# A Mamba scan inside a two-layer trunk: the decay work behind the last Silu, the first scan step two items later, another bank for the first feature, the last group's items in a new order

## The chip, the cores and the metric

One core of a Trainium2 chip runs the whole program in one launch. The metric is device microseconds (us) of one execution; lower is better. Engines are named as the profile names them: PE (TensorE, its weight loads as PEld), DVE (VectorE), ACT (ScalarE), POOL (GpSimd) and SP (SyncE, which here only issues transfers). Each engine takes its instructions in one fixed order, and an instruction that waits holds up all behind it.

## What is computed

The reference is a trunk of two pre-norm layers on 256 tokens of width 2048, in float32: a Mamba-2 mixer, an MLP, a dilated attention, an MLP and a last norm. The change touches the Mamba mixer alone. Cut to what matters:

```python
zxbcdt = u @ w_in                                 # z 4096, xbc 6144, dt 64 columns
xbc = silu(causal_depthwise_conv(xbc, conv_w, conv_b))
xs, bm, cm = split(xbc)                           # 8 groups of 512, 128 and 128 columns
L  = segsum_exp(dt * A)                           # decays inside a chunk of 128 tokens
cb = einsum("bclgn,bcsgn->bcgls", cm, bm)
y  = einsum("bcgls,bgjcls,bcsgjp->bclgjp", cb, L, x) + y_off     # y_off: state of the chunk before
y  = (y + d_skip * xs) * silu(z)
y  = per-group rms norm of y * norm_w
return y @ w_out
```

## The kernel before, in words

**Weights.** Each weight unit is a tile of 128x2048 floats (1 MB). SP loads it into a raw buffer, ACT copies it with rounding into `wh`, the high part (L267), DVE subtracts the two into `wl`, the low part (L268), and PE multiplies with both (`fetch`, L219). There are three pairs of `wh`/`wl`, used in turn. So the `wh` of a unit may be written only when PE has finished the unit three places before, and a raw buffer is loaded again only when the `wl` made from it is done. From the third group on plain units share two raw buffers; the third is tile A, and there is a tile B.

**Groups.** The mixer works through eight groups of heads. A group has six features (`c0` to `c3` for x, `c4` for B, `c5` for C; 32 matmuls each, L295), and four quarters of its gate (`z0` to `z3`, 24 matmuls each, L330 to L332). A feature's bank is emptied (`c_ux`, `c_ut`), convolved with four taps (`c_ua`, L533 and L535) and put through a Silu (`c_uo`, L538). The gate's two banks are read by the two `zs` Silus (L613).

**Scan.** Each group's scan has three steps, and the steps of one group lie in different places. `first` (item `f`, L616) fetches the rows of cumulated decays (`ab<-acs_rows`, a transfer issued by ACT), multiplies B with C on PE (`cb`, L633), takes Abs of each of 16 blocks with the head's offset as bias (L643) and Exp of both halves (L648) on ACT, multiplies them with `cb` on DVE (L650), and transposes the features (`xt`, `bt`) with five products on DVE (`xdt`, `xd`, `xdd`). `second` runs in the next group: `y` (L693) up to the first half's output, and `Y` with the state's part (`yo`). `third` (`t`) transposes the result. Item `p` makes from two groups the seven operands (`op`, L754, L755) of a seven-product scheme for the output projection.

**Output projection.** Items `1` to `7` are those seven products (12 matmuls, L785). Each adds up in a bank that DVE then adds to the residual `x_res` (L793). Products `5` and `3` use bank 3, `1`, `6`, `7` and `4` bank 2. Their weights are made in tiles A and B by adding transfers issued by POOL, except for `1`, `3` and `2`, which SP loads. Items `o60` to `o73` are the plain projection of the last two groups.

**Order.** The table `GROUP_ORDER` (L50) writes out by hand the order of the items in each group. From group 3 on, PE's order is pinned to it (`put_in_order`, L553), as is the chain of all `wh` and `wl`. The other instructions on ACT and DVE are placed by a scheduler that works with modelled times; `tc.issue_after` forbids it to place an instruction ahead of another.

Of the kernel before, what the change touches and what calls it, by code (L numbers as in the profile page):

```python
# [10 lines left out]
AF = mybir.ActivationFunctionType  # L11
# [5 lines left out]
NH = S // P  # L17
# [5 lines left out]
HG = 8  # L23
# [17 lines left out]
def alibi_slope(g, h):  # L41
# [6 lines left out]


GROUP_ORDER = {  # L50
    1: "c0 c1 c2 c3 c4 y Y c5 z0 z1 z2 z3 t f",
    2: "c0 c1 c2 y Y c3 c4 c5 t f z0 p z1 z2 z3",
    **{g: "c0 c1 1 c2 y c3 Y 5 c4 3 c5 t 6 z0 7 f z1 2 z2 4 z3" + " p" * (g % 2 == 0) for g in range(3, 7)},
    7: "c0 c1 1 c2 y c3 Y 5 c4 3 c5 t 6 z0 7 f z1 2 z2 4 z3",
    8: "1 o60 y o61 Y 5 o62 3 o63 t 6 7 o70 2 o71 4 o72 o73",
}
GROUP_ORDER = {g: order.split() for g, order in GROUP_ORDER.items()}

# [55 lines left out]
def hybrid_trunk_kernel(ctx: ExitStack, tc: tile.TileContext, a: dict, out: bass.AP):  # L114
    nc = tc.nc
# [24 lines left out]
    def bank(name, among):  # L140
        k = banks_of.use(banks_of.peek(among))
        return psum.tile([P, 512], F32, tag=f"b{k}", name=name, bufs=1)
# [264 lines left out]
    def ssm(nx):  # L407
# [9 lines left out]
        for j in range(4):  # L417
            n = KT if j == 0 else 0
            if j == 0:
                t, sq = sp.tile([P, n + 4 * S], F32, tag="B", name="xt0_0", bufs=1), None  # L420
                g0 = t[:, :KT]
            else:
                t, sq = (sp.tile([P, 4 * S], F32, tag="op", name=f"xt{k}_{j}", bufs=7) for k in range(2))
# [37 lines left out]
        sm = {}  # L461
# [61 lines left out]
        y3, silus = {}, []  # L523
# [29 lines left out]
        def put_in_order(make):  # L553

            if not fixed[0]:
                return make()
            with tc.issue_after(latest[0]):
                return make()
# [5 lines left out]
        class Group:  # L564
# [30 lines left out]
            def features(self, u):  # L595
                g, name = self.g, f"c{self.g}_{u}"
                unit = lambda made=None: cols_units([("in", g, u)], xs, [name], first=(u != 1 if g >= 3 else u < 2),
                                                     made=made)[0]
                ps = put_in_order(lambda: unit([bank(name, (0, 1))] if g >= 3 else None))
                self.ch.append(conv_tile(g, u, ps))  # L600

            def gate(self, q):
# [13 lines left out]
            def first(self):  # L616
                g, ch = self.g, self.ch
                ab = sp.tile([P, NH, HG, P], F32, tag="ab", name=f"ab{g}", bufs=1)
                rows = sm["scratch"][:, g * HG * P:(g + 1) * HG * P]
                nc.scalar.dma_start(ab.rearrange("p m h t -> p m (h t)"),  # L620
                                    rows.unsqueeze(0).to_broadcast([P, NH, HG * P]))
                hs = slice(g * HG, (g + 1) * HG)
                bT, cT = ch[4], ch[5]

                def bc(v):
                    return v.unsqueeze(2).to_broadcast([P, HG, HD])

                def heads(t):
                    return t.rearrange("p (h d) -> p h d", h=HG)

                ps = sm_bank(f"cb{g}")
                halves = [slice(m * P, (m + 1) * P) for m in range(NH)]
                small(lambda: [nc.tensor.matmul(ps[:, t], bT[:, t], cT[:, t], start=(t.start == 0), stop=True,  # L633
                                                skip_group_check=True) for t in halves])
                cb = sp.tile([P, NH, P], F32, tag="cb", name=f"cbm{g}", bufs=1)
                nc.vector.tensor_tensor(cb, ps[:, :S].rearrange("p (m l) -> p m l", m=NH),
                                        tri[:, None, :].to_broadcast([P, NH, P]), ALU.mult)

                es = [ab[:, m] for m in range(NH)]
                for m in range(NH):  # L640
                    for h in range(HG):
                        av = sm["less"][:, m, g * HG + h:g * HG + h + 1]
                        nc.scalar.activation(es[m][:, h], es[m][:, h], AF.Abs, bias=av)  # L643
                with ExitStack() as order:
                    for ins in silus[-2:]:
                        order.enter_context(tc.issue_after(ins))
                    for m in range(NH):
                        nc.scalar.activation(es[m], es[m], AF.Exp, scale=-1.0)  # L648
                for m in range(NH):
                    nc.vector.tensor_tensor(es[m], es[m], cb[:, m:m + 1, :].to_broadcast([P, HG, P]),  # L650
                                            ALU.mult)

                xdt, xd = [], []
                for m in range(NH):
                    ps = sm_bank(f"xt{g}_{m}")
                    small(lambda: [nc.tensor.transpose(ps[:, c * P:(c + 1) * P], ch[c][:, halves[m]], ident)
                                   for c in range(4)])
                    t = sp.tile([P, GW], F32, tag="xdt", name=f"xdt{g}_{m}", bufs=2)
                    nc.vector.tensor_tensor(heads(t), heads(ps), bc(sm["dt"][:, m, hs]), ALU.mult)
                    xdt.append(t)  # L660
                    t = sp.tile([P, GW], F32, tag="xd", name=f"xd{g}_{m}", bufs=2)
                    nc.vector.tensor_tensor(heads(t), heads(ps), bc(dskip[:, hs]), ALU.mult)
                    xd.append(t)
                    if m == 0:
                        t = sp.tile([P, GW], F32, tag="yo", name=f"xdd{g}", bufs=1)
                        nc.vector.tensor_tensor(heads(t), heads(ps), bc(sm["ddt"][:, hs]), ALU.mult)
                        xdd = split(t, GW, "xdd", f"xdds{g}")
                ps = sm_bank(f"bt{g}")
                small(lambda: [nc.tensor.transpose(ps[:, :P], bT[:, :P], ident)])
                btok = split(ps[:, :P], P, "bs", f"btok{g}")  # L670
                cs = split(cT[:, P:], P, "bs", f"cs{g}")
                self.kept = es, xdt, xd, xdd, btok, cs
# [72 lines left out]
        def operands(pair):  # L745


            left, right = slice(0, P), slice(P, S)
            y0, y1 = y3[2 * pair], y3[2 * pair + 1]
            a11, a21, a12, a22 = y0[:, :, left], y0[:, :, right], y1[:, :, left], y1[:, :, right]  # L750
            of = {k: sp.tile([P, 4, 2, P], F32R, tag="op", name=f"op{pair}_{k}", bufs=7) for k in "1536724"}

            def parts(k, t):
                nc.scalar.activation(of[k][:, :, 0], t, AF.Copy)  # L754
                nc.vector.tensor_tensor(of[k][:, :, 1], t, of[k][:, :, 0].bitcast(F32), ALU.subtract)  # L755

            parts("1", a11)
            parts("4", a22)
            nc.vector.tensor_tensor(a22, a21, a22, ALU.subtract)
            parts("5", a22)  # L760
            nc.vector.tensor_tensor(a21, a11, a21, ALU.add)
            nc.vector.scalar_tensor_tensor(a11, a22, -1.0, a11, op0=ALU.mult, op1=ALU.subtract)
            parts("2", a12)
            nc.vector.scalar_tensor_tensor(a12, a12, -1.0, a11, op0=ALU.mult, op1=ALU.subtract)
            parts("3", a12)
            parts("6", a11)
            parts("7", a21)
            return of
# [24 lines left out]
            nc.vector.tensor_tensor(xc, xc, ps, op)  # L793

        def plain(g, j):
            banks = [bank(f"wo{g}_{j}_{m}", (0, 1)) for m in range(NH)]
            lhs = lambda k, part, t: y3[g][t.start // P][:, k, part]
            put_in_order(lambda: rows_unit(banks, [("out", g, j)], lhs, 0, 4, 512, True, True))
            add_residual(banks, j)
            if g == 7:  # L800
                step_on(nx, j)
# [9 lines left out]
        for g, order in GROUP_ORDER.items():  # L811
            before = cur
            cur = Group(g)
            fixed[0] = g >= 3
            for item in order:
                if item[0] == "c":
                    cur.features(int(item[1]))
                elif item[0] == "z":
                    cur.gate(int(item[1]))
                elif item == "y":  # L820
                    rest = before.second()
                    next(rest)
                elif item == "Y":
                    next(rest, None)
                elif item == "t":
                    before.third()
                elif item == "f":
                    cur.first()
                elif item == "p":
                    of[(g - 2) // 2] = operands((g - 2) // 2)  # L830
                elif item[0] == "o":
                    plain(int(item[1]), int(item[2]))
                else:
                    product((g - 3) // 2, item, "ab"[(g - 3) % 2])
# [437 lines left out]
```

## Time and profile before

| what | value |
|---|---|
| median of 3 runs | 2603.98 us (2600.7 to 2606.12) |
| profiled execution, its own time | 2602.75 us |
| span of its trace | 2601.0 us |
| mean granted TensorE clock | 0.985 |
| busy PE, DVE, ACT | 2532.7, 2058.6, 1602.2 us |
| Mamba mixer, from the start to about | 757 us |

A row of the timeline gives start, duration, engine, line, operation and tiles, and in brackets how long the engine had been idle and what ended that. A row that ends in x4 stands for four instructions in a line. The granted clock is the share of full speed that PE was given.

### The profile page before, as it was taken

Reading aid. Unit: us, or ns where it says so; the run is one execution under the profiler, and the core shown is the slowest. Engines: PE = TensorE matmul, PEld = TensorE weight load, DVE = VectorE, ACT = ScalarE, POOL = GpSimd, SP = SyncE. Lnnn points to the kernel's source line nnn. Section 1 sums busy time; section 2 is a strip of 40 time slices with the busy share of each in tenths; the row PEclk is TensorE's granted clock in tenths of the full one; section 3 lists DMA queues with packets and bytes.
Section 4 is the critical chain, followed back from the end, with each engine's and each line's share of the span. In section 5 each row is a group of like instructions: output and inputs, shape, how many; then the busy total and the mean of one; then the engine's idle time right before and its main releaser. Section 6 shows DMA issues by size and latency. Waiting matters only on the chain.

```text
span 2601.0 us, 34411 instructions
## 1 busy us (share of the span) xinstructions
PE 2532.7 (97%) x13737; PEld 2176.2 (84%) x13737; DVE 2058.6 (79%) x2296; ACT 1602.2 (62%) x1991; POOL 119.8 (5%) x143
## 2 busy tenths in 40 slices
PE   9998989987999999999999999999999999999998
PEld 7887867776788888888888999999988888888887
DVE  8777777677678988889886766667767988899885
ACT  7776566566456656666665666666656666666664
POOL 0000000000000000000000000000000000000001
PEclk9999989998999999999999999999999999999999
DMA  8556757666668888898875444455458888998883
GB/s 310 192 186 173 247 179 208 197 207 210 168 250 220 259 258 252 248 262 255 254 217 203 170 168 164 162 173 172 166 218 228 248 252 248 258 267 253 252 235 140
DMA packets 83696, 567.43 MB, mean 218 GB/s; under 512 B 9296, under 2 KB 9936, under 8 KB 20048
## 3 DMA queue, kind: packets, MB, share of 16 engines
q1 hardware_dynamic: 65232, 441.50, 47.0%
q0 software_dynamic: 15552, 113.25, 22.4%
q10 hardware_dynamic: 2752, 10.49, 1.2%
q8 instruction: 108, 1.77, 0.3%
q14 instruction: 52, 0.43, 0.0%
HBM read 563.04 MB, written 2.16 MB: 217 GB/s over the span
## 4 chain that ended last, share of the span: by engine, by line
PE 77%; DMA 2%; ACT 1%; DVE 1%; issue 0%; ACTq 0%; POOLq 0%; POOL 0%
PE h L295 27%; PE qk L295 10%; PE pxb L1089 6%; PE pxa L1089 6%; PE pwb L1089 3%; PE pwa L1089 3%; PE v L330 2%; PE v L331 2%; PE v L332 2%; PE c L295 2%; PE pzb L1089 1%; PE pza L1089 1%; PE d L330 1%; PE d L331 1%; PE d L332 1%; PE s L860 1%
## 5 line engine op out<-in xcount | busy, mean ns | idle before, releaser
L268 DVE TENSOR_TENSOR wl<-raw,wh 128x2048 fp32r<-128x2048 f32 (+4 forms) x368 | 796.7, 2167 | 299.4 <-ACT wh L267 298.2
L267 ACT ACTIVATE wh<-raw 128x2048 fp32r<-128x2048 f32 (+4 forms) x368 | 669.8, 1822 | 397.9 <-PE h L295 80.8
L295 PE MATMUL h<-xn,wh 128*128 128x512 f32 x2048 | 690.1, 392 | 0.0
L295 PE MATMUL h<-xn,wl 128*128 128x256 f32 x2048 | 555.5, 280 | 0.0
L295 PEld LDWEIGHTS h<-xn,wh 128*128 128x128 f32 x2048 | 376.4, 188 | 76.1
L295 PEld LDWEIGHTS h<-xn,wl 128*128 128x128 f32 x2048 | 385.0, 188 | 13.8
L295 PE MATMUL c<-xn,wh 128*128 128x512 f32 x768 | 263.5, 394 | 0.3 <-ACT wh L267 0.2
L295 PE MATMUL qk<-xn,wh 128*128 128x512 f32 x768 | 259.3, 393 | 0.0
L295 PE MATMUL c<-xn,wl 128*128 128x256 f32 x768 | 211.4, 283 | 5.0 <-ACT zs L613 2.5
L295 PE MATMUL qk<-xn,wl 128*128 128x256 f32 x768 | 209.2, 283 | 0.0
L295 PEld LDWEIGHTS c<-xn,wh 128*128 128x128 f32 x768 | 142.2, 188 | 31.8 <-ACT wh L267 2.6
L295 PEld LDWEIGHTS qk<-xn,wh 128*128 128x128 f32 x768 | 141.1, 188 | 28.8
L295 PEld LDWEIGHTS c<-xn,wl 128*128 128x128 f32 x768 | 144.0, 188 | 10.6 <-DVE wl L268 3.5
L295 PEld LDWEIGHTS qk<-xn,wl 128*128 128x128 f32 x768 | 141.4, 188 | 3.6 <-issue 1.2
L267 ACT ACTIVATE wh<-Ab 128x2048 fp32r<-128x2048 f32 x42 | 80.4, 1915 | 72.6 <-DMA Ab<-in_w 60.0
L268 DVE TENSOR_TENSOR wl<-Ab,wh 128x2048 fp32r<-128x2048 f32 x42 | 96.1, 2287 | 14.0 <-ACT wh L267 14.0
L267 ACT ACTIVATE wh<-Aa 128x2048 fp32r<-128x2048 f32 x42 | 80.3, 1913 | 38.6 <-DMA Aa<-in_w 30.6
L268 DVE TENSOR_TENSOR wl<-Aa,wh 128x2048 fp32r<-128x2048 f32 x42 | 96.1, 2288 | 7.4 <-ACT wh L267 7.3
L331 PE MATMUL z<-wl,xn 128*128 128x512 f32 x256 | 101.0, 394 | 0.0
L330 PE MATMUL z<-wh,xn 128*128 128x512 f32 x256 | 101.0, 399 | 0.0
L332 PE MATMUL z<-wh,xn 128*128 128x512 f32 x256 | 100.7, 394 | 0.0
L1038 ACT ACTIVATE r<-r 128x256 f32<-128x256 f32 x128 | 52.2, 411 | 73.0 <-DVE r L1037 73.0
(471 smaller groups left out, 4998.5 us busy)
## 6 DMA issues: line engine op xcount, KB each, us to landing
raw<-in_w SPq DMA_DIRECT2D x172, 1024.0 KB, 5.2
raw<-in_w_in SPq DMA_DIRECT2D x74, 1024.0 KB, 4.9
raw<-in_w_qk SPq DMA_DIRECT2D x48, 1024.0 KB, 4.8
Aa<-in_w POOLq DMA_DIRECT2D x28, 1024.0 KB, 9.6
Ab<-in_w POOLq DMA_DIRECT2D x28, 1024.0 KB, 9.9
raw<-in_w_v SPq DMA_DIRECT2D x32, 768.0 KB, 4.3
A<-in_w_out POOLq DMA_DIRECT2D x18, 1024.0 KB, 8.9
raw<-in_w_out SPq DMA_DIRECT2D x14, 1024.0 KB, 7.4
```

The source lines that it names most:

```text
L267: high[i] = nc.scalar.activation(wh[:, c], raw[:, c], AF.Copy).ins
L268: low[i] = nc.vector.tensor_tensor(wl[:, c], raw[:, c], wh[:, c].bitcast(F32), ALU.subtract).ins
L295: latest[0] = nc.tensor.matmul(ps[:, :n], (wh, wl)[part][:, kt * P:(kt + 1) * P], xs[:, kt, :, :].rearrange("p a t -> p (a t)")[:, :n], st ...
L330: nc.tensor.matmul(banks[m][:, :n], hi, wh[:, c], start=st, stop=False)
L331: nc.tensor.matmul(banks[m][:, :n], hi, wl[:, c], start=False, stop=False)
L332: latest[0] = nc.tensor.matmul(banks[m][:, :n], lo, wh[:, c], start=False, stop=sp).ins
L860: latest[0] = nc.tensor.matmul(ps[:, at:at + nk], qa[g, hl][:, qs], k[g, hl][:, :nk], start=first and at == 0, stop=not first, skip_group_ ...
L1038: nc.scalar.activation(t, t, AF.Square)
L1089: latest[0] = nc.tensor.matmul(ps, lhs(i, part), w[:, n], start=(first and i == 0 and part == 0 and w is wh), stop=(i == 3 and part == 1), ...
```

## The change

Six edits, all in the Mamba mixer:

1. The 16 Abs of `first` move into the block that may only be issued behind the last two Silus of the features, each half's Abs ahead of its Exp.
2. From group 3 to 7 item `f` stands behind `z1` and `2` and no longer ahead of them.
3. `Y` stands behind `5` in groups 3 to 7. In group 1 both halves of the second step stand behind `c5`, in group 2 `Y` behind `c3`.
4. From group 3 on `c0` uses bank 3 and no longer one of banks 0 and 1; so does the first bank of `o60`.
5. Group 8 has its items in another order: `y` right behind `1`, `t` ahead of `3`, and products between the plain units.
6. The operands of `p` may only be issued behind the last Silu.

```diff
-    **{g: "c0 c1 1 c2 y c3 Y 5 c4 3 c5 t 6 z0 7 f z1 2 z2 4 z3" + " p" * (g % 2 == 0) for g in range(3, 7)},
+    **{g: "c0 c1 1 c2 y c3 5 Y c4 3 c5 t 6 z0 7 z1 2 f z2 4 z3" + " p" * (g % 2 == 0) for g in range(3, 7)},
...
-    8: "1 o60 y o61 Y 5 o62 3 o63 t 6 7 o70 2 o71 4 o72 o73",
+    8: "1 y o60 Y o61 5 o62 t 3 o63 6 o70 7 o71 2 4 o72 o73",
...
-                ps = put_in_order(lambda: unit([bank(name, (0, 1))] if g >= 3 else None))
+                ps = put_in_order(lambda: unit([bank(name, (0, 1) if u else (3,))] if g >= 3 else None))
...
-                for m in range(NH):
-                    for h in range(HG):
-                        av = sm["less"][:, m, g * HG + h:g * HG + h + 1]
-                        nc.scalar.activation(es[m][:, h], es[m][:, h], AF.Abs, bias=av)
                 with ExitStack() as order:
                     for ins in silus[-2:]:
                         order.enter_context(tc.issue_after(ins))
                     for m in range(NH):
+                        for h in range(HG):
+                            av = sm["less"][:, m, g * HG + h:g * HG + h + 1]
+                            nc.scalar.activation(es[m][:, h], es[m][:, h], AF.Abs, bias=av)
                         nc.scalar.activation(es[m], es[m], AF.Exp, scale=-1.0)
...
-            banks = [bank(f"wo{g}_{j}_{m}", (0, 1)) for m in range(NH)]
+            banks = [bank(f"wo{g}_{j}_{m}", (3,) if g == 6 and j + m == 0 else (0, 1)) for m in range(NH)]
...
-                    of[(g - 2) // 2] = operands((g - 2) // 2)
+                    with tc.issue_after(silus[-1]):
+                        of[(g - 2) // 2] = operands((g - 2) // 2)
```

**Place one.** ACT's order in group 4, from the transfer of the decay rows to the high part of product `3`'s weights, which are in tile B. Before:

```order
L620 DMA ab_3183<-acs_rows 128x2x1024
L710 ACTIVATE ssq_junk,sq_0_2885<-xd_0_2514 128x512
L643 ACTIVATE ab_3183<-ab_3183,acs 128x128 x4
L533 ACTIVATE c_2a<-upad_191,vecs 128x256
L643 ACTIVATE ab_3183<-ab_3183,acs 128x128 x9
L313 ACTIVATE c_3x<-c_3_2893 128x256
L538 ACTIVATE c_1o<-c_1a,vecs 128x256
L713 ACTIVATE xd_0_2514<-xd_0_2514,rq_0_2887 128x512
L267 ACTIVATE wh_2961<-B_2960 128x2048
```

The same stretch of ACT in group 4 in the changed kernel:

```order
L620 DMA ab_3232<-acs_rows 128x2x1024
L709 ACTIVATE ssq_junk,sq_0_2885<-xd_0_2563 128x512
L533 ACTIVATE c_2a<-upad_191,vecs 128x256
L267 ACTIVATE wh_2946<-B_2945 128x2048
L313 ACTIVATE c_3x<-c_3_2893 128x256
```

The 13 Abs, which read what the transfer brings, no longer stand between the transfer and the weights of `3`, and three further pieces now follow those weights.

**Place two.** ACT's order in group 4 around the last feature's Silu, `c_5o`. The first row of both pieces is the high part of item `2`; the next `wh` from a raw buffer is that of `z2`, and the one from tile A (L262) that of item `4`. Before:

```order
L267 ACTIVATE wh_3165<-raw_3164 128x2048
L538 ACTIVATE c_4o<-c_4a,vecs 128x256
L754 ACTIVATE op_5_3374<-yT_3099 128x4x128
L754 ACTIVATE op_2_3378<-yT_3099 128x4x128
L267 ACTIVATE wh_3242<-raw_3241 128x2048
L538 ACTIVATE c_5o<-c_5a,vecs 128x256
L648 ACT_TABLE_LOAD
L648 ACTIVATE ab_3183<-ab_3183 128x1024 x2
```

In the changed kernel:

```order
L267 ACTIVATE wh_3165<-raw_3164 128x2048
L538 ACTIVATE c_4o<-c_4a,vecs 128x256
L538 ACTIVATE c_5o<-c_5a,vecs 128x256
L646 ACTIVATE ab_3232<-ab_3232,acs 128x128 x16
L753 ACTIVATE op_1_3373<-yT_2396 128x4x128
L267 ACTIVATE wh_3184<-raw_3183 128x2048
L753 ACTIVATE op_4_3379<-yT_3099 128x4x128
L647 ACT_TABLE_LOAD
L647 ACTIVATE ab_3232<-ab_3232 128x1024 x2
L262 ACTIVATE wh_3214<-A_2671 128x2048
```

`c_5o` now stands ahead of the high part of `z2`, and all 16 Abs behind `c_5o`. The high part of `4` has the Abs, the table load and both Exps ahead of it. In odd groups, which have no `p`, the two `op` rows are missing.

DVE's order at the same place, from the low part of `z2` on. Before:

```order
L268 TENSOR_TENSOR wl_3243<-raw_3241,wh_3242 128x2048
L636 TENSOR_TENSOR cbm_3188<-cb_3185,vecs 128x256
L659 TENSOR_TENSOR xdt_0_3215<-xt_0_3210,dta 128x512
L662 TENSOR_TENSOR xd_0_3217<-xt_0_3210,vecs 128x512
L666 TENSOR_TENSOR xdd_3219<-xt_0_3210,dec 128x512
```

In the changed kernel:

```order
L268 TENSOR_TENSOR wl_3185<-raw_3183,wh_3184 128x2048
L754 TENSOR_TENSOR op_4_3379<-yT_3099,op_4_3379 128x4x128
L792 TENSOR_TENSOR x_res<-x_res,qz0b 128x512
L636 TENSOR_TENSOR cbm_3237<-cb_3234,vecs 128x256
L658 TENSOR_TENSOR xdt_0_3264<-xt_0_3259,dta 128x512
L661 TENSOR_TENSOR xd_0_3266<-xt_0_3259,vecs 128x512
L665 TENSOR_TENSOR xdd_3268<-xt_0_3259,dec 128x512
L658 TENSOR_TENSOR xdt_1_3278<-xt_1_3273,dta 128x512
L661 TENSOR_TENSOR xd_1_3280<-xt_1_3273,vecs 128x512
L758 TENSOR_TENSOR yT_3099<-yT_2396,yT_3099 128x4x128
L649 TENSOR_TENSOR ab_3232<-ab_3232,cbm_3237 128x1024 x2
L263 SCALAR_TENSOR_TENSOR wl_3215<-A_2671,wh_3214 128x2048
```

Both kernels put the products of `f` ahead of the low part of `4` (L263). Since `f` now comes two items later on PE, it comes right ahead of `z2`, with `4` the next item but one.

More of the change, by code (lines that the diff above doesn't have):

```diff
@@ L50 @@
 GROUP_ORDER = {
-    1: "c0 c1 c2 c3 c4 y Y c5 z0 z1 z2 z3 t f",
-    2: "c0 c1 c2 y Y c3 c4 c5 t f z0 p z1 z2 z3",
-    **{g: "c0 c1 1 c2 y c3 Y 5 c4 3 c5 t 6 z0 7 f z1 2 z2 4 z3" + " p" * (g % 2 == 0) for g in range(3, 7)},
-    7: "c0 c1 1 c2 y c3 Y 5 c4 3 c5 t 6 z0 7 f z1 2 z2 4 z3",
-    8: "1 o60 y o61 Y 5 o62 3 o63 t 6 7 o70 2 o71 4 o72 o73",
+    1: "c0 c1 c2 c3 c4 c5 y z0 Y z1 z2 z3 t f",
+    2: "c0 c1 c2 y c3 Y c4 c5 t f z0 p z1 z2 z3",
+    **{g: "c0 c1 1 c2 y c3 5 Y c4 3 c5 t 6 z0 7 z1 2 f z2 4 z3" + " p" * (g % 2 == 0) for g in range(3, 7)},
+    7: "c0 c1 1 c2 y c3 5 Y c4 3 c5 t 6 z0 7 z1 2 f z2 4 z3",
+    8: "1 y o60 Y o61 5 o62 t 3 o63 6 o70 7 o71 2 4 o72 o73",
 }
```

## The prediction

> **What bounds the kernel now.** The windows of the profile come first: group 3 to 6 (each from the item behind `c2` to the same place one group later), group 7, group 8, the rest. The columns are the stretch, its us, the busy time of PE, PEld, DVE, ACT and POOL, the granted clock, DMA's share and GB/s.
>
> ```profile
> 220.07:313.32 93.25, 83.40 (x466) 69.36 (x464) 68.46 (x76) 57.29 (x74) 5.14 (x7) 0.96 0.72 219
> 313.32:409.06 95.74, 84.89 (x465) 71.36 (x464) 71.63 (x85) 58.25 (x77) 4.92 (x7) 0.93 0.66 198
> 409.06:498.45 89.39, 83.68 (x465) 69.88 (x464) 66.00 (x75) 55.24 (x72) 4.98 (x7) 0.96 0.71 212
> 498.45:593.50 95.05, 84.83 (x465) 71.23 (x464) 71.66 (x85) 58.18 (x77) 5.00 (x7) 0.93 0.66 199
> 593.50:683.11 89.61, 75.70 (x394) 61.93 (x392) 58.26 (x73) 50.44 (x69) 4.48 (x6) 0.89 0.61 182
> 683.11:760.00 76.89, 74.61 (x406) 61.59 (x405) 60.99 (x72) 43.93 (x61) 4.49 (x6) 0.98 0.72 222
> 760.00:2601.00 1841.00, 1831.46 (x9872) 1590.51 (x9870) 1486.28 (x1571) 1118.80 (x1315) 86.18 (x94) 1.00 0.73 222
> ```
>
> PE is the bound everywhere. From 760 on it idles 9.5 of 1841 us, so nothing is to be had there, and the change doesn't touch it. In groups 3 to 7 it idles 5.7 to 13.9 us a group, and the clock falls to 0.89 to 0.96. The waits of PE between 220 and 683 say on what (total, times, longest):
>
> ```profile
> PE cb L633 <- ACT c_5o L538: 17.7, 3, 6.2
> PE qw0a L785 <- DVE x_res L793: 5.7, 1, 5.7
> PE qw0b L785 <- ACT wh L267: 3.5, 1, 3.5
> PE qw2a L785 <- ACT wh L267: 3.4, 1, 3.4
> ```
>
> Two places, then: `cb` at item `f`, and product `3` (the `qw` rows, once a group). ACT stands behind both. At `3` it waits for the decay rows, five times 5.3 us; this is group 4:
>
> ```profile
> ACT ab L643 <- DMA ab<-acs_rows: 26.3, 5, 6.3
> ```
>
> ```profile
> 326.94 1.28 ACT L643 ACTIVATE ab<-ab,acs 128x128 f32<-128x128 f32 x4 [5.37 <-DMA ab<-acs_rows]
> ...
> 332.44 1.90 ACT L267 ACTIVATE wh<-B 128x2048 fp32r<-128x2048 f32 x1
> ```
>
> ```profile
> 334.39 0.80 PE L785 MATMUL qw0b<-wh,op 128*128 128x512 f32 x1 [3.48 <-ACT wh L267]
> ```
>
> The Abs wait 5.37, then 13 of them run, and only then comes `wh` of `3`, for which PE has idled 3.48. At `f`, ACT waits 2.83 for a load before it makes `wh` of `z2`, and `c_5o` stands behind that:
>
> ```profile
> 362.25 1.91 ACT L267 ACTIVATE wh<-raw 128x2048 fp32r<-128x2048 f32 x1 [2.83 <-DMA raw<-in_w_in]
> 364.06 0.49 ACT L538 ACTIVATE c_5o<-c_5a,vecs 128x256 f32<-128x256 f32 x1
> 364.57 1.28 ACT L648 ACT_TABLE_LOAD   x1
> 365.87 2.00 ACT L648 ACTIVATE ab<-ab 128x1024 f32<-128x1024 f32 x2
> ```
>
> ```profile
> 364.61 1.22 PE L633 MATMUL cb<-c_5o,c_4o 128*128 128x128 f32 x4 [5.85 <-ACT c_5o L538]
> ```
>
> A gap also costs behind its end. Product `3` of group 3, behind its gap, takes from 245.06 to 249.68, where an undisturbed product takes 2.75:
>
> ```profile
> 245.06 0.76 PE L785 MATMUL qw0a<-wh,op 128*128 128x512 f32 x1 [5.70 <-DVE x_res L793]
> ...
> 249.28 0.40 PE L785 MATMUL qw0a<-wh,op 128*128 128x512 f32 x1
> ```
>
> ```profile
> 585.37 2.75 PE qx2a L785 x12
> 588.12 5.55 PE c L295 x32
> ```
>
> (The last two are from the chain of waits: a product is 2.75, a unit of 32 matmuls 5.55.) I put this slow stretch at 1.7 us a gap.
>
> **What is lost before.** A group without gaps needs group 3's busy time less one slow stretch, 83.4 - 1.7 = 81.7; group 7, whose clock of 0.89 speaks for two or three, 75.7 - 2.5 x 1.7 = about 71.5. Window less content: 11.6, 14.0, 7.7, 13.4 and 18.1, together 64.8 us.
>
> **The change, part by part.**
>
> *Abs behind the last Silu.* Nothing is added, and the transfer of the rows is issued at the same place on ACT; SP's order stays as it is. But ACT no longer meets the transfer ahead of `3`. The old order had the Abs at 326.94 and `c_5o` at 364.06; with `c_5o` earlier by the count below, some 25 us of these 37 are left for the transfer to land, which in the old order was late by 5.4. So `wh` of `3` comes about 10 us earlier than wanted, and the gap at `3` goes. The 16 Abs now stand behind `c_5o`, for 4.8 us, as group 1 has them in a line:
>
> ```profile
> 97.72 4.80 ACT L643 ACTIVATE ab<-ab,acs 128x128 f32<-128x128 f32 x16 [1.33 <-DMA ab<-acs_rows]
> ```
>
> *`f` two items later.* `cb` needs `c_5o`, and this no longer stands behind `wh` of `z2`. To see what is late next I count from the end of `c5`'s matmuls. PE, where nothing waits: `t` 0.9, `6` 3.6, `z0` 9.1, `7` 11.8, `z1` 17.3, `2` 20.0, `f` (1.7, the row below and nine transposes) 21.7, `z2` 27.2, then `4`.
>
> ```profile
> 453.99 0.71 PE L633 MATMUL cb<-c_5o,c_4o 128*128 128x128 f32 x4
> ```
>
> ACT: `wh` of `2` may start when `z0` is done, 9.1, and ends at 11.0; `c_4o`, `c_5o` at 11.9, eight us ahead of `f`; Abs until 16.7; `wh` of `z2` 18.6; table and both Exps 3.3, until 21.9; `wh` of `4` 23.8. In even groups `op_1` and `op_4` add 1.1: 24.9. DVE:
>
> ```profile
> 370.72 2.35 DVE L650 TENSOR_TENSOR ab<-ab,cbm 128x1024 f32<-128x1024 f32 x2
> 372.99 0.68 DVE L544 TENSOR_TENSOR xdds<-xdd,xdds 128x512 fp32r<-128x512 f32 x1
> 373.60 0.68 DVE L755 TENSOR_TENSOR op<-yT,op 128x512 fp32r<-128x512 f32 x1
> 375.38 2.29 DVE L263 SCALAR_TENSOR_TENSOR wl<-A,wh 128x2048 fp32r<-128x2048 f32 x1 [1.10 <-ACT wh L262]
> ```
>
> `wl` of `z2` ends at 20.9 and one `x_res` at 21.5. From `f`'s end, 21.7, `cbm` 0.3 and five products of 0.6 (the spacing of such operations) give 24.9, the `ab` products 27.2, `wl` of `4` 29.4. PE wants that at 27.4, with `4`'s second matmul: **a new gap of 2.0 us**. In even groups two operations more on DVE and the `op` on ACT make it 31.1: a gap of 3.7, with 1.7 behind it. In group 7 `z3` comes late by some 1.5. What else gets tight: `z2` has 0.2 to 0.7 to spare; the next group's `c1` about 0.3, since its raw buffer comes free only with `wl` of `z3`; `t` 2.0, as the second half's norm now runs behind `wh` and `wl` of `6` and POOL's `rq` behind the issue for `4`.
>
> *The bank of the first feature* frees `c0` from the `zs` that a wait of 1.4 shows at most, and puts `c1` on that bank one unit (5.55) later. Bank 3 was last read by `x_res` of `3`, long done. `Y` behind `5` gives the state's chain on DVE one product (2.75) more time and takes as much from `t`, whose slack of 2.0 has it in already. Both are in the count above.
>
> *Groups 1 and 2, operands of `p`.* PE had 30 of `c5`'s 32 matmuls ahead of `y` in group 1 already; `ab`'s chain there is unchanged. I put these at nothing, plus or minus 2.
>
> *Group 8.* Two matmuls into product `2` PE waits for the scan's last transposes, and the pairs behind run at 1.05 instead of 0.62:
>
> ```profile
> 715.02 0.47 PE L785 MATMUL qx2b<-wh,op 128*128 128x512 f32 x1 [2.28 <-ACT y3t L741]
> ...
> 716.30 1.05 PE L785 MATMUL qx2b<-wh,op 128*128 128x512 f32 x2
> ```
>
> With `y` and `t` earlier that goes: 2.28 + 1.7 = 4.0.
>
> **The sum.** Lost after: 2.0, 5.4, 2.0, 5.4, 1.5 = 16.3, against 64.8: a gain of 48.5, with group 8 52.5. From the execution's own 2602.75 that gives 2550.2. The slacks of 0.2 to 0.7 won't all hold; I allow 6 us, three gaps of about 2. That is 2556 in the profile's time; the median shown, 2603.98, lies 1.2 above the profiled execution, so **2557**.
>
> [...] The row at 715.02 says that 2.28 of idling already brings the slow clock. [...]
>
> **The rivals.** 0.2% (5 us) is about what a measurement of this kernel can tell from no change.
>
> *Loads become the bound* (0.22). The groups ask for the same 19 MB or so each (about 200 GB/s over 95 us) in less time.
>
> ```profile
> raw<-in_w_in SPq DMA_DIRECT2D x74, 1024.0 KB, 4.9
> ...
> raw<-in_w_out SPq DMA_DIRECT2D x14, 1024.0 KB, 7.4
> ```
>
> If `c1`'s load lands in 9 and not in 5 to 7, `c1` is late by 2, with 1.7 of slow clock: 5 x 3.7 = 18.5 more, **2575**. For it: no slack there. Against: the DMA share, 0.72 at most.
>
> *Only the gap at `f` closes* (0.05). If `3` is held by something else behind the Abs (ACT waits for DVE's `xd` just before), the gain is 17.7 and three slow stretches, 23: **2581**. Against: `wh` of `3` follows the Abs directly.
>
> *New gaps where the old were* (0.05). If the gap at `4` grows to about 9, the time is the same, **2604**.
>
> *Slower* (0.08). Ahead of everything on ACT now stands `wh` of `2`: `c_5o`, the Abs, `z2`'s weights, the Exps and `4`'s are behind it.
>
> ```profile
> ACT wh L267 <- DMA raw<-in_w_out: 2.7, 1, 2.7
> ```
>
> If that load lands late, all of it slides into PE's path. With 46.5 gained over five groups, it decides from 9.3 us a group; at 12 it is 60 - 46.5 = 13.5 on top, **2617**. For it: one such wait is there. Against: it is 2.7, and the load takes 7.4.
>
> **The numbers.** The forecast has 0.60 and its own range is 2543 to 2568: down by the even groups' gaps staying short of the slow clock and the allowance unused, up by a gap of 2 at `c1` in three groups. With the first two rivals the range is **2540 to 2590**, which leaves out the last two and a little below. Faster 0.60 + 0.22 + 0.05 = **0.87**, same **0.05**, slower **0.08**.
>
> **What would show it.** In the changed kernel's profile: windows of about 84 (odd) and 87 (even) us; ACT's wait for the decay rows gone; `cb` without a wait; a new wait of PE at `4` for DVE's `wl` from tile A, 2 to 4 us; the clock at 0.96 or more; no gap in product `2` of group 8. I am wrong if `cb` still waits, if `3` does, or if `z2` or `c1` wait for their weights each time.

## The result, and the profile after

The changed kernel takes 2563.14 us (median of 4 runs, 2561.19 to 2565.63) against 2604.85 us (4 runs, 2600.7 to 2606.12): ratio 0.9843, with a 95% interval of 0.9826 to 0.986. It is faster by 1.6%, 41.7 us. The forecast was 2557, in a range of 2540 to 2590.

The windows of the profile after, cut at the same places as before: group 2, groups 3 to 6, group 7, and group 8 to the last matmul of the output projection. The columns are those of the windows above.

```profile
155.76:224.25 68.49, 65.84 (x393) 56.05 (x392) 54.03 (x75) 44.91 (x71) 2.80 (x3) 0.98 0.51 162
224.25:311.10 86.85, 81.61 (x465) 68.25 (x464) 65.03 (x73) 55.98 (x73) 6.94 (x6) 1.00 0.75 228
311.10:396.73 85.63, 81.06 (x465) 68.34 (x464) 72.08 (x85) 56.59 (x78) 6.67 (x6) 1.00 0.72 214
396.73:484.35 87.62, 82.72 (x465) 69.50 (x464) 65.45 (x74) 55.34 (x72) 6.68 (x6) 0.98 0.73 222
484.35:571.73 87.38, 82.44 (x465) 69.44 (x464) 72.08 (x85) 58.13 (x79) 6.54 (x6) 0.98 0.72 218
571.73:638.81 67.08, 64.12 (x370) 53.68 (x368) 57.41 (x72) 47.68 (x69) 6.68 (x6) 1.00 0.73 217
638.81:710.90 72.09, 71.22 (x384) 58.16 (x383) 58.53 (x66) 42.45 (x56) 3.74 (x5) 1.00 0.77 232
```

The same stretches before that the prediction did not show, group 2 and group 8 to the end of the output projection:

```profile
156.16:220.07 63.91, 63.91 (x393) 54.72 (x392) 52.51 (x73) 44.61 (x70) 2.41 (x3) 1.00 0.54 172
683.11:751.84 68.73, 66.45 (x357) 54.37 (x356) 56.01 (x64) 39.70 (x54) 3.77 (x5) 0.98 0.70 208
```

Groups 3 to 6 shrink from 373.4 us (220.07 to 593.50) to 347.5, by 25.9. Groups 7 and 8 together (their border moves, since `y` comes earlier in group 8) go from 158.3 to 139.2, by 19.2. Up to group 3, 4.2 us are lost: group 2 goes from 63.91 to 68.49, with 0.4 gained ahead of it. The rest gains 0.7. That is 41.6, the difference of the spans (2601.0 and 2559.4).

What PE waits for between 210 and 680 in the changed kernel, in total, times and longest:

```profile
PE yT L727 <- ACT xd L712: 10.3, 5, 3.3
PE qx1b L784 <- DVE wl L263: 2.4, 1, 2.4
PE qx0b L784 <- DVE wl L263: 2.3, 1, 2.3
PE bt L668 <- DVE x_res L792: 2.3, 2, 1.1
PE qx1a L784 <- DVE wl L263: 1.8, 1, 1.8
PE qx0a L784 <- DVE wl L263: 1.7, 1, 1.7
PE qx2b L784 <- DVE wl L268: 1.7, 1, 1.7
```

`cb` no longer waits, product `3` at most 0.2, and the new waits at product `4` (the `qx` rows with `wl` L263, one in each of groups 3 to 6) are there, as forecast. The last row is not product `4` but product `1` of group 8, the item right behind `z3` of group 7. The largest wait, at item `t` (`yT`), was not forecast. In group 4 it comes about so; DVE first, then POOL, then ACT and PE:

```profile
334.60 0.15 DVE L342 TENSOR_SCALAR rt<-sq 128x1 f32<-128x1 f32 x1
334.66 2.28 DVE L268 TENSOR_TENSOR wl<-raw,wh 128x2048 fp32r<-128x2048 f32 x1
```

```profile
334.05 0.86 POOL L253 DMA_DIRECT2D A<-in_w_out  x1 [7.89 <-DVE wl L268]
334.83 2.53 POOL L343 TENSOR_TENSOR rq<-rt,halfpow 128x1 f32<-128x1 f32 x1
```

```profile
337.40 0.72 ACT L712 ACTIVATE xd<-xd,rq 128x512 f32<-128x512 f32 x1 [3.48 <-POOL rq L343]
```

```profile
338.17 0.98 PE L727 MATMUL yT<-ident,xd 128*128 128x128 f32 x7 [1.08 <-ACT xd L712]
```

`rq` is one element in each partition. The second half's takes 2.53 to 2.87 us in groups 3 to 7 of the changed kernel, and all others 0.54 to 1.05. Here it starts 0.17 us into a low part of 2.28 us and ends 0.4 us after it. ACT waits 3.48 us for it, and PE for ACT.

### The profile page after: what moved, and what is told of

Read it like the earlier page. It is cut to its first block, busy times and chain, and to the rows that moved or that the text cites. A ratio compares the mean times of both kernels' runs of the same rounds, so it can differ in the third digit from the quotient of the medians.

```text
span 2559.4 us, 34405 instructions
## 1 busy us (share of the span) xinstructions
PE 2518.8 (98%) x13737; PEld 2166.9 (85%) x13737; DVE 2057.7 (80%) x2296; ACT 1598.3 (62%) x1991; POOL 128.9 (5%) x143
## 4 chain that ended last, share of the span: by engine, by line
PE 74%; DVE 2%; DMA 1%; ACT 1%; issue 1%; POOL 0%; ACTq 0%; POOLq 0%; DVEq 0%
PE h L295 28%; PE qk L295 11%; PE pxb L1089 6%; PE pxa L1089 6%; PE pwb L1089 3%; PE pwa L1089 3%; PE v L332 2%; PE v L330 2%; PE v L331 2%; PE pzb L1089 1%; PE pza L1089 1%; PE d L331 1%; PE d L330 1%; PE d L332 1%; DMA A<-in_w_out 1%; PE s L860 1%
## 5 line engine op out<-in xcount | busy, mean ns | idle before, releaser
L267 ACT ACTIVATE wh<-Aa 128x2048 fp32r<-128x2048 f32 x42 | 80.3, 1913 | 40.3 <-DMA Aa<-in_w 32.1
```

The lines of the kernel that those rows point to most:

```text
L267: high[i] = nc.scalar.activation(wh[:, c], raw[:, c], AF.Copy).ins
```

## The experiments

Each batch ran with the kernel before on the same chip; its medians there were 2602.95, 2600.7 and 2602.36, so times from different batches compare to about 2 us; where that matters, the ratios are given too.

### Which edit takes which wait away

The first three undo all but one or two edits. `e_abs` is the kernel before with the first edit alone:

```diff
-                for m in range(NH):
-                    for h in range(HG):
-                        av = sm["less"][:, m, g * HG + h:g * HG + h + 1]
-                        nc.scalar.activation(es[m][:, h], es[m][:, h], AF.Abs, bias=av)
...
                     for m in range(NH):
+                        for h in range(HG):
+                            av = sm["less"][:, m, g * HG + h:g * HG + h + 1]
+                            nc.scalar.activation(es[m][:, h], es[m][:, h], AF.Abs, bias=av)
                         nc.scalar.activation(es[m], es[m], AF.Exp, scale=-1.0)
```

> The kernel before with the first edit alone: the 16 Abs behind the last Silu, each half's ahead of its Exp; the item table, banks and operands as before. Theory A (one stall feeds the other): with the Abs gone from ahead of product 3, the last Silu c_5o is also placed ahead of z2's weights on ACT, so both of PE's waits go by this edit alone, the 26.0 us at product 3 with about 7 us of slow clock and most of the 17.7 at cb with its 5; what is left at cb is about 1 us a group, since f still comes ahead of z1 and 2. Time about 2556 (2548 to 2566). Theory B (two stalls, one edit each): the wait at cb stays, 5 to 6 us in three groups; time about 2572 (2567 to 2578).

It takes **2546.72 us** (0.9782, interval 0.9766 to 0.9798): 16 us faster than the whole change. This is ACT in group 4, around the last Silu:

```profile
339.96 1.92 ACT L267 ACTIVATE wh<-raw 128x2048 fp32r<-128x2048 f32 x1 [2.49 <-PE z L332]
341.78 1.13 ACT L753 ACTIVATE op<-yT 128x512 fp32r<-128x512 f32 x2
342.82 0.49 ACT L538 ACTIVATE c_5o<-c_5a,vecs 128x256 f32<-128x256 f32 x1
343.22 4.78 ACT L646 ACTIVATE ab<-ab,acs 128x128 f32<-128x128 f32 x16
347.91 1.90 ACT L267 ACTIVATE wh<-raw 128x2048 fp32r<-128x2048 f32 x1
```

`c_5o` stands right behind the high part of `2` and the operands, ahead of `z2`'s high part (347.91), though `f` is where it was. The longest of what PE waits for from 215 to 640 in this kernel:

```profile
PE bt L668 <- DVE y3t L741: 6.5, 1, 6.5
PE yo L548 <- DVE state L544: 2.0, 1, 2.0
PE cb L633 <- ACT c_5o L538: 1.7, 3, 0.7
```

The wait at `cb` is down from 17.7 to 1.7 by the Abs alone. Groups 4 to 6 take 81.5, 80.3 and 81.5 us; in group 5 PE never idles:

```profile
386.38:466.69 80.31, 80.31 (x465) 68.36 (x464) 66.02 (x76) 55.07 (x72) 4.96 (x6) 1.00 0.78 236
```

That is theory A, and more than it had put down. `e_f2` is the kernel before with `f` moved and nothing else:

```diff
-... t 6 z0 7 f z1 2 z2 4 z3
+... t 6 z0 7 z1 2 f z2 4 z3
```

> The kernel before with item f two later in groups 3 to 7 and nothing else. Both theories: the wait at cb goes (17.7 us and three slow stretches, 23 us in all), product 3 goes on waiting for its high part, 2.5 to 5.7 us a group, with ACT waiting for the decay rows as before. Time about 2582 (2577 to 2588). If it comes out near 2604, the new place of f gives back at product 4 what it gains at cb.

It takes **2592.82** (0.9959, 0.9946 to 0.9972): a gain of 10, not 23. The longest of PE's waits from 215 to 660:

```profile
PE bt L669 <- DVE x_res L793: 12.1, 4, 5.1
PE qw0a L785 <- DVE x_res L793: 5.7, 1, 5.7
PE qw2a L785 <- ACT wh L267: 3.8, 1, 3.8
```

The waits at `3` stay, as expected, and `cb` no longer waits; but a new wait, 12.1 us for the bank of `bt`, comes with `f`: product `2` uses a bank of the same set, and right behind `2` this bank still waits for DVE's addition to `x_res`. Neither theory had this. In group 4 `c_5o` runs at 364.77, still behind `z2`'s high part, as in the kernel before (364.06): by itself `f`'s move doesn't bring `c_5o` forward, it lets PE come to `cb` later. `e_abs_f2` has both edits:

> The kernel before with the first two edits together: Abs behind the last Silu, f two items later. Theory A: f's move has nothing left to gain and brings the wait at product 4 (1.7 to 2.4 us a group in the changed kernel), so this is slower than the Abs alone, by 5 to 12 us: 2561 to 2572. Theory B: the gains add, 33 and 23 us less 10 at product 4: about 2559, and 10 us or more faster than the Abs alone.

It takes **2558.51** (0.983, 0.9816 to 0.9845), 11.8 us slower than the Abs alone: theory A again. `f`'s new place has next to nothing left to gain in groups 3 to 6; in its profile these are the longest of PE's waits from 215 to 660. The first, the first feature's wait for the gate's Silu, isn't in the whole change from group 4 on, where this feature has bank 3; no run takes that edit alone:

```profile
PE c L295 <- ACT zs L613: 7.2, 2, 4.2
PE z L331 <- DVE wl L268: 2.3, 3, 1.0
PE yo L548 <- DVE state L544: 2.2, 1, 2.2
PE qx1a L784 <- DVE wl L263: 1.6, 1, 1.6
```

### The loss in group 2

In the changed kernel the first feature of group 3 waits for the Silu of group 2's gate, and its 64 matmuls with the next feature's take 13.0 us, where they take 11.3 elsewhere. `a_bank3` lets this feature alone use the old banks:

```diff
-                ps = put_in_order(lambda: unit([bank(name, (0, 1) if u else (3,))] if g >= 3 else None))
+                ps = put_in_order(lambda: unit([bank(name, (0, 1) if u or g == 3 else (3,))] if g >= 3 else None))
```

> The changed kernel, but group 3's first feature takes bank 0 or 1 as before; groups 4 to 7 keep bank 3 for it. The changed kernel loses 4.2 us between the scan of group 2 and that of group 3, with a wait of 2.65 us of the first feature for the Silu of group 2's gate. Theory G1 (the new bank makes it: bank 3 is one of the gate's two banks in group 2): wait gone, 2563.1 - 4.2, about 2559. Theory G2 (the Silu is late whatever the bank, behind the Abs and the operands on ACT): wait and time stay, 2563, give or take 2.

It takes **2557.52** (0.9826, 0.9811 to 0.9841), 4 to 6 us under the changed kernel by the ratios and by the times (the intervals just overlap), and the wait, of which this is the row in the changed kernel, is gone:

```profile
203.10 0.50 PE L295 MATMUL c<-xn,wl 128*128 128x256 f32 x2 [2.65 <-ACT zs L613]
```

G1: in group 2 the gate may use any of banks 0 to 3, and the fixed bank 3 of group 3's first feature is one that it still holds. From group 4 on the gate uses banks 0 and 1, and bank 3 is free.

### The wait at t

`c_abs_Y` adds to `e_abs` the move of `Y` alone:

```diff
-... y c3 Y 5 c4 3 c5 t ...
+... y c3 5 Y c4 3 c5 t ...
```

> The kernel with the Abs behind the last Silu alone (2546.7), plus Y behind product 5 in groups 3 to 7. Theory R (Y's new place makes the wait at item t): on DVE the second half's rt then comes right ahead of a low part of weights, and POOL's rq, which stands behind a transfer's issue, takes 2.5 us beside that low part and not 0.7, as in the changed kernel; PE waits at t for xd in all five groups, 1 to 3.3 us each, 10 us in all and up to 4 of slow clock: 2553 to 2561. Rival (the wait at t comes from f's new place, which shifts DVE's work): no wait at t, 2547, give or take 2.

It takes **2560.32** (0.9843, 0.9829 to 0.9856), 13.6 us over `e_abs` (16 by the ratios). The second `rq` of group 4, on POOL:

```profile
331.67 2.54 POOL L343 TENSOR_TENSOR rq<-rt,halfpow 128x1 f32<-128x1 f32 x1
```

It takes 2.54 in all five groups (0.56 or 0.72 in `e_abs`, where three short taps follow `rt` on DVE). So far theory R. But the cost lies elsewhere than it said:

```profile
PE cb L633 <- ACT c_5o L538: 11.8, 3, 4.5
PE yT L727 <- ACT xd L712: 4.0, 5, 3.1
```

Only group 3 waits long at `t`. From there on `rq` ends 25.4 us after the group's start, when PE reaches `t` at 25.7, and `t` waits 0.2. What costs is ACT's order in groups 4, 6 and 7, here in group 4:

```profile
348.24 1.91 ACT L267 ACTIVATE wh<-raw 128x2048 fp32r<-128x2048 f32 x1 [0.61 <-DMA raw<-in_w_in]
350.06 0.49 ACT L538 ACTIVATE c_5o<-c_5a,vecs 128x256 f32<-128x256 f32 x1
```

`c_5o` stands behind `z2`'s high part again, as in the kernel before; in even groups two operands of `p` (1.1 us) are ahead of both. In `e_abs`, where the same operands stand ahead of `c_5o` but `z2`'s high part doesn't, `cb` waits only 0.7. So `Y`'s move gives the scheduler another order and brings the first wait back; why it chooses this order stays open. `a_f0` below also has the sixth edit, the operands behind the last Silu. There `c_5o` follows `c_4o` directly in the even groups, and `cb` waits in group 7 alone, but other edits are in `a_f0` too, and no run has the sixth alone.

`a_rq` takes the changed kernel and computes `rt` of the second half on POOL:

```diff
-                    root(rq, sq, GW, f"rt{g}_{m}")
+                    t = work.tile([P, NH], F32, tag="root", name=f"rt{g}_{m}", bufs=2)
+                    (nc.gpsimd if m and g >= 2 else nc.vector).tensor_scalar(t[:, :1], sq, 1.0 / GW, EPS, ALU.mult, ALU.add)
+                    nc.gpsimd.tensor_tensor(rq, t[:, :1], halfpow[:, :1], ALU.pow)
```

> The changed kernel with the second half's rt (from group 3 on) on POOL, where rq follows it at once, ahead of the issue of product 4's transfer; nothing else moves but one Silu on ACT. Theory R: rq no longer waits for DVE's queue nor for the issue, xd is ready some 2 us earlier, the waits at t (10.3 us in five groups) go down to under 2 in all: 2563 - 8 to 12 = 2551 to 2555. If rt or rq still takes 2 us and more, it is since a low part runs on DVE at the same time. Rival (xd is late for its square on ACT, not for rt and rq): waits stay, 2562.

It takes **2553.95** (0.9819, 0.9806 to 0.9833), 6 to 9 us under the changed kernel by the ratios and by the times, and the waits at `t` are gone. POOL in group 4:

```profile
328.61 1.97 POOL L712 TENSOR_SCALAR rt<-sq 128x1 f32<-128x1 f32 x1 [5.68 <-ACT ssq_junk L709]
330.67 0.56 POOL L713 TENSOR_TENSOR rq<-rt,halfpow 128x1 f32<-128x1 f32 x1
```

`rt`, 0.19 in group 8, now takes 1.97 in group 4 beside the low part of tile A, and `rq` behind that low part 0.56. The long time beside a low part stays, now with `rt`, but two waits fewer lie ahead of `xd`. With `t` earlier, the bank of `bt` becomes the largest wait, 7.9 us in all where it had been 2.3.

### The table of groups 3 to 7, undone in the changed kernel

`a_f0` puts `f` back, `a_Y` puts `Y` back, `a_Yf0` both:

```diff
-... y c3 5 Y c4 3 c5 t 6 z0 7 z1 2 f z2 4 z3
+... y c3 5 Y c4 3 c5 t 6 z0 7 f z1 2 z2 4 z3
```

> The changed kernel with f back ahead of z1 and 2 in groups 3 to 7 (Y stays behind product 5). If costs simply carry over from the kernel with Abs and Y alone (2560.3), less 6.4 for group 8's order, plus 4.2 for the bank in group 2: about 2558, with the waits at product 4 gone and cb waiting for c_5o, 3.6 to 4.5 us in the even groups and group 7. If f's place costs by itself what it does without the other edits (11.8), it would be 2551.

> The changed kernel with Y back ahead of product 5 in groups 3 to 7 (f stays two items later). Theory R: the waits at t (10.3 us) go, since rt no longer stands ahead of a low part; product 4 goes on waiting 1.7 to 2.4 a group; about 2551 (2548 to 2555).

> The changed kernel with the item table of groups 3 to 7 as before, so Y and f both back; Abs, banks, group 8, operands and groups 1 and 2 as changed. If the two moves of the table are what the change loses against the Abs and group 8 alone (2540.4), and the bank in group 2 the rest (4.2): 2545 (2541 to 2548). If the other edits (operands, groups 1 and 2) cost something as well, over 2548.

They take **2547.33** (0.9786, 0.977 to 0.9802), **2549.97** (0.9797, 0.9783 to 0.9812) and **2543.8** (0.9778, 0.9763 to 0.9792). `a_Y` and `a_Yf0` came as expected, `a_f0` faster than either number. In `a_f0` the waits at `cb` in the even groups, which are part of the first number, aren't there. By these times and ratios, `f`'s move costs 6 us with `Y` in its old place and 15 to 16 with `Y` moved; `Y`'s costs 3.5 (the runs overlap) and 12 to 13. Each makes the other's worse. The profiles show how: in the changed kernel DVE comes to the first half of `y` 5.4 to 7.5 us after the start of groups 4 to 7, in `a_f0` after 4.3 to 4.7. In the changed kernel a low part from tile A, whose transfer lands late, comes first; in group 5 (start 396.73):

```profile
397.54 1.91 ACT L267 ACTIVATE wh<-A 128x2048 fp32r<-128x2048 f32 x1 [4.03 <-DMA A<-in_w_out]
399.48 2.29 DVE L268 TENSOR_TENSOR wl<-A,wh 128x2048 fp32r<-128x2048 f32 x1 [3.38 <-ACT wh L267]
```

POOL issues this transfer 9.0 to 10.6 us ahead of the group's start, in `a_f0` 12.7 to 13.3, and there DVE is done with this low part before the start. How `f`'s place delays the issue wasn't followed further. `rq` ends 26.3 to 28.4 us after the start instead of 25.4, and PE wants `t` at 25.7. In `a_f0` that leaves of the wait at `t` 3.3 us in group 3 and 0.2 in the others.

### A version that beats both

`c_abs_g8` is `e_abs` with the new order of group 8. `c_best` moves `f` two items later in group 7 as well, the one group where `e_abs` waits there (6.5 us for a bank):

```diff
-    7: "c0 c1 1 c2 y c3 Y 5 c4 3 c5 t 6 z0 7 f z1 2 z2 4 z3",
-    8: "1 o60 y o61 Y 5 o62 3 o63 t 6 7 o70 2 o71 4 o72 o73",
+    7: "c0 c1 1 c2 y c3 Y 5 c4 3 c5 t 6 z0 7 z1 2 f z2 4 z3",
+    8: "1 y o60 Y o61 5 o62 t 3 o63 6 o70 7 o71 2 4 o72 o73",
```

> The Abs alone (2546.7), plus the new order of group 8. The wait of 2.36 us in product 2 of group 8 and its slow clock go: 2546.7 - 4.0 = 2542.7. Rival: the new order of the last group only moves its waits, 2547 give or take 2.

> The Abs alone, plus the new order of group 8, plus f two items later in group 7 alone, where f waits 6.5 us for a bank that the last piece of the transposed output holds. That wait goes, some slow clock with it, and product 4's wait of 1.7 comes: 2542.7 - 5 = about 2538 (2535 to 2541), faster than both kernels. Rival: f's place costs in group 7 what it does in the others (12 us in five groups), 2543 or more.

They take **2540.37** (0.9766, 0.9753 to 0.978) and **2537.45** (0.9756, 0.9743 to 0.9769). Group 8's order is worth 6.4 us by the times and 4.2 by the ratios (0.9782 and 0.9766, with intervals that overlap), where I had put down 4.0. In `c_best` the wait of 6.5 for the bank goes, but the one at `o61` for an addition to the residual grows from 0.8 to 3.6. `c_best4` adds bank 3 for the first bank of `o60`:

```diff
-            banks = [bank(f"wo{g}_{j}_{m}", (0, 1)) for m in range(NH)]
+            banks = [bank(f"wo{g}_{j}_{m}", (3,) if g == 6 and j + m == 0 else (0, 1)) for m in range(NH)]
```

> The fastest kernel so far (Abs behind the last Silu, new order of group 8, f two items later in group 7; 2537.5), plus the changed kernel's bank 3 for the first bank of o60, and nothing else. There PE waits 3.62 us at o61 for the addition of o60 to the residual, which holds the bank. The wait goes, with up to 1.7 of slow clock: 2537.5 - 3.6 to 5.3 = 2532 to 2534. Rival: the next wait behind it takes its place, 2536 to 2538.

**2534.82** (0.9742, 0.9727 to 0.9756): the wait goes down from 3.62 to 1.99 and not to nothing, as the addition for the second bank is late as well. Its ratio's interval overlaps that of `c_best`, so this last step is not certain. The longest of what PE still waits for from 215 to 660:

```profile
PE wo L330 <- DVE x_res L337: 2.0, 1, 2.0
PE cb L633 <- ACT c_5o L538: 1.4, 2, 0.7
```

## Why the prediction was right, and where not

The direction, the place and the size held: 41.7 us of gain against 47 forecast. Step by step:

- **Product 3.** Right. The wait for the decay rows left ACT's way, and `3` has no gap over 0.2.
- **cb.** The wait went, but the step that credits it to `f`'s new place failed. `e_abs` shows that the Abs's move alone puts `c_5o` ahead of `z2`'s high part and takes the wait from 17.7 to 1.7. `f`'s move alone (`e_f2`) ends the wait too, but puts 12.1 at `bt` in its place. I took `c_5o`'s new place from the order of the whole change and did not ask which edit had made it; so I also held `f`'s move for a gain, where behind the Abs's move it costs 6 to 16 us in groups 3 to 7, and gains 3 in group 7 alone.
- **Product 4.** Right in groups 3 to 6: 2.0, 3.7, 2.0 and 3.7 were forecast; 1.74, 2.34, 1.75 and 2.36 measured. In the even groups PE has already waited 1.14 and 1.13 for the bank of `bt`, for an addition in the same queue on DVE, which makes 3.5 there. The sum puts 1.7 us of slow clock behind the gap in even groups and none in odd ones, which was an estimate of mine that the run did not bear out: the 3 us behind the gaps of groups 3, 4 and 5 have a granted clock of 1.00, those of group 6 one of 0.50. In group 7, where 1.5 was forecast at `z3`, neither `4` nor `z3` waits. The 1.67 lost behind it, at product `1` of group 8, has another cause: its weights come through tile A, and ACT waits 3.66 for that load. Together 12.1 against 12.9.
- **t.** The slack of 2.0 was wrong. It had `rq` at its 0.7 of before; beside a low part it takes 2.5 to 2.9, and in groups 4 to 7 DVE comes to `y` 1.1 to 3.2 us later than before as well. 10.3 us of waits; the allowance of 6 covered about half.
- **Group 2.** Put at nothing, plus or minus 2; it lost 4.6. I had looked at bank 3 from group 3 on, where it is free, and not at its first use, where group 2's gate still holds it.
- **Group 8.** The size held, 4.0 forecast and 4.2 to 6.4 in `c_abs_g8` against `e_abs`; the cause was misread. The row at 715.02 is the first matmul of product `7`, not one in product `2` (which adds up in `qz` tiles). `7` goes on in the bank of `6`, which stands right ahead of it, and starts only when DVE has added that bank to `x_res` (until 714.87); in `e_abs` the row names it:

```profile
660.24 0.47 PE L784 MATMUL qx2b<-wh,op 128*128 128x512 f32 x1 [2.36 <-DVE x_res L792]
```

The new order puts `o70` between `6` and `7`. That `y` and `t` come earlier is not shown to matter here.
- **The rivals.** Loads never became the bound: no wait for a feature's weights is among PE's waits from group 3 to 7. But ACT waits 25.0 us from 210 to 650 for transfers into tile A, 6.8 in the kernel before; the late `y` and the wait at product `1` of group 8 stand behind some of these. The slower rival needs a late load for `2`, and PE waits for `2` in no group. New gaps did come where PE had none, but at 10.3 and 12.1 us in all they are far from the 65 lost before.

In sums, groups 3 to 6 gained 25.9 where the terms give 31.9 without the allowance, and groups 7 and 8 19.2 where they give 20.6; 4.2 were lost up to group 3, which was put at nothing. Of these 11.6 the allowance covers 6. That the time came within 6 us of the forecast is in part luck: the allowance was meant for `z2` and `c1`, which never wait, and it met the misses at `t` and in group 2.

## What to carry to other kernels

An edit that takes a long wait out of one engine's queue moves what is behind it, too: before a second edit is made for the next wait, the order or the profile with the first alone shows whether that wait is still there. Where a scheduler makes the order, that place can also come back with an edit that doesn't name it, as `c_5o`'s did in `c_abs_Y`. Here one of six edits is worth more than all six together. A slack is worked out with the durations that the operations will have beside their new neighbours (for `rq` beside a low part 2.5 to 2.9 us here, and not the 0.7 of before). And a buffer that is free in the steady state is looked at once more at its first use.

## What the runs showed of the hardware

**POOL beside DVE.** In the changed kernel `rq`, one element a partition, takes 2.5 to 2.9 us when it starts 0.17 us into a low part, and 0.71 to 0.73 when it starts as far into a tap of 0.48 (L535), which reads two tiles; for both it ends some 0.4 us behind that operation (0.75 in group 3). Beside an addition that reads one tile and a bank it takes 0.55, much as with no operation of DVE beside it (0.54). Two more, with several operations beside them, take 0.88 and 1.05:

```profile
656.38 0.68 DVE L337 TENSOR_TENSOR x_res<-wo,x_res 128x512 f32<-128x512 f32 x1
656.54 0.55 POOL L343 TENSOR_TENSOR rq<-rt,halfpow 128x1 f32<-128x1 f32 x1 [4.74 <-DVE rt L342]
```

In `a_rq` `rt` takes 0.19 in group 8 and 1.7 to 2.3 beside a low part, and ends with it. The transfer's issue on POOL takes 0.85 to 0.90 us with or without a low part beside it (once 1.03). The low part and the tap read two tiles, the addition one. No run put a long operation that reads one tile in the low part's place, so whether the number of tiles read is what makes `rq` longer is not shown.

**The clock after a gap.** Two gaps of the same length, at product `4` of group 4 and of group 6 in the changed kernel, end differently:

```profile
369.19 0.51 PE L784 MATMUL qx0b<-wl,op 128*128 128x512 f32 x1 [2.34 <-DVE wl L263]
369.54 0.64 PE L784 MATMUL qx0b<-wh,op 128*128 128x512 f32 x2
```

```profile
542.77 0.80 PE L784 MATMUL qx1b<-wl,op 128*128 128x512 f32 x1 [2.36 <-DVE wl L263]
543.36 1.06 PE L784 MATMUL qx1b<-wh,op 128*128 128x512 f32 x2
```

After 2.34 us the next pair takes 0.64, and the granted clock of the 3 us behind the gap is 1.00; after 2.36 us the pair takes 1.06, and the clock is 0.50. At `t`, the 3 us behind 3.31 us of idling in group 3 have a clock of 1.00, and those behind 3.13 in group 5 one of 0.59:

```profile
254.34 0.98 PE L727 MATMUL yT<-ident,xd 128*128 128x128 f32 x7 [3.31 <-ACT xd L712]
```

```profile
425.93 1.27 PE L727 MATMUL yT<-ident,xd 128*128 128x128 f32 x7 [3.13 <-ACT xd L712]
```

So in these four gaps, of 2.3 to 3.3 us, it is not the length alone that decides; what else does is not shown. The prediction put the slow clock behind each even group's gap at `4`, and was right in one of two. Its reading of the row at 715.02, that 2.28 us of idling brings the slow clock, fits the kernel before, where the 3 us from there on have a clock of 0.69, but not the gap of 2.34 in group 4 here.
